# Scores of 64-wide heads by pairs on the two row halves of TensorE, even and odd heads in two banks

## The chip, the cores and the metric

The kernel runs on one core of one Trainium2 chip. The metric is the device time of one execution in microseconds (us), the median of three runs. The inputs are laid out on the host into the order in which the weights are read; everything that the reference computes is done in one launch.

## The reference

Two transformer-like blocks of two layers each follow each other on a sequence of 256 rows of width 1024, all in float32. Four of the attentions have heads of 64; the change touches three of them.

```python
# first block, per layer
y = hybrid_mixer(x, ...)        # A: chunked relative-position attention, 8 heads of 64
                                # B: latent attention, 8 heads of 64+32 (query/key 96 wide)
                                # C: forgetting attention, 8 heads of 64 (+2 columns of decay: 66)
x = layer_norm(alpha * x + y)
x = layer_norm(alpha * x + memory_cross_attention(x, mem, ...))   # 4 heads of 128
x = layer_norm(alpha * x + swiglu_ffn(x, ...))                    # hidden 2816

# second block, per layer; scale, shift and gate come from a modulation vector c
x = x + 0.5 * g1 * swiglu(norm(x))
h = norm(x)
o_a = stick_breaking(qa, ka, va)        # 4 heads of 64
o_d = dilated_mixture(qd, kd, vd)       # 4 heads of 64
o_h = hgrn2(qh, fh, ih, gh)             # 4 heads of 128, a gated linear recurrence
x = x + g2 * (concat(o_a, o_d, o_h) @ w_out)
x = x + 0.5 * g3 * swiglu(norm(x))

# the attentions that the change touches: A, stick_breaking, dilated_mixture
s = einsum('qhd,khd->hqk', q, k) * 64 ** -0.5 + bias_or_mask
p = softmax(s)                          # stick_breaking: exp of a cumulative sum instead
o = einsum('hqk,khd->qhd', p, v)
```

## The kernel before

The 256 rows are two threads of 128 (t = 0 and t = 1). Thread 0 runs ahead, thread 1 follows some weight tiles behind, so that each weight is loaded and split once and used by both. Every wide product is done in three float32r products: weights and activations are split into a rounded part and the rest (tiles `wh`, `wl`; for part of the weights both in the pool `E`; activations as two tiles of pool `S`), and `mm3` makes three products of 128x512 for each 128 rows of weight. Short float32 products (scores, values, the recurrence) are made directly; in the trace each of them is two MATMUL records and two LDWEIGHTS records, here called passes. A transpose is one record.

Nothing is issued in the order in which it is written. The program is recorded (`Recorder.add`), each operation gets a cost (`cost`, line 227), and a list scheduler (`listed`, line 282) sets the order of every engine: it works out a due time for every operation backwards from the order of TensorE's work, in which the duration of an operation that is not TensorE's is multiplied by `SLACK` (line 131), and then takes on each engine the ready operation that is due first, if the tiles it writes have room. Each thread has one PSUM bank `m` for the wide products and three banks `a` for everything else. So the scores of a head can be put between the wide products of the other thread, one matmul at a time.

`cost` gives a transpose 110 ns (`FP32`, line 524) and any other float32 product 220 ns.

The scores of heads of 64 (`scores`, line 770; called from `exponentials`, line 795, for attention A and the dilated attention, and from `stick`, line 1292): the transposed keys hold two heads in one block of 128 rows, the even head in rows 0 to 63, the odd one in rows 64 to 127. The queries (`queries`, line 855) are copied by ScalarE, half a tile at a time, into a tile of pool `E` that has one block per head and zeros in the other head's half (`zeroed`, line 863, four memsets on GpSimd), so that each score matmul runs over all 128 rows of the array, with the whole block of keys moving. Four score blocks of 128x128 fill one bank: four heads at t = 0, two heads with two key blocks each at t = 1. In the page these matmuls are `a<-S,E` with 128 rows and 128 columns; B and C have rows of 96 and 66 (`a<-S,S`) and are not touched.

The values (`values`, line 782) transpose the four probability blocks into one bank, ScalarE copies them, and then four matmuls `a<-T,S` each make 64 columns: the output of an even head stands in PSUM partitions 0 to 63, that of an odd head in 64 to 127. The softmax loop (line 825) holds one group of four blocks back while the next one's scores are made.

Of the kernel before, what the change touches and what calls it, by code (L numbers as in the profile page):

```python
# [130 lines left out]
SLACK = 1.5  # L131
# [16 lines left out]
class Recorder:  # L148
# [78 lines left out]
    def cost(self, op, name, out, src, kw):  # L227
# [9 lines left out]
        if op.eng == "PE":  # L237
            return (4.7 + 0.4406 * n, 0) if src[1].dtype == F32R else ((1 if name == "transpose" else 2) * FP32, 0)
# [290 lines left out]
class Program:  # L529
# [240 lines left out]
    def scores(self, t, nh, qT, kT):  # L770

        n = 4 // (t + 1)
        for b in range(0, nh, n):
            ps = self.ps()
            g = list(range(b, b + n))
            for i, h in enumerate(g):
                for u in range(t + 1):
                    o = (i * (t + 1) + u) * 128
                    self.nc.tensor.matmul(ps[:, o:o + 128], qT(h), kT(u, h), start=True, stop=True)
            yield g, ps  # L780

    def values(self, t, g, p, v, o, dv):


        nc = self.nc
        ps = self.blocks_T(p, 4)
        pT = self.tile("T", [128, 512])
        nc.scalar.copy(pT, ps)
        steps = [(i, u) for i in range(len(g)) for u in range(t + 1)]
        for i, u in sorted(steps, key=lambda k: k[::-1]) if dv < 128 else steps:  # L790
            h = g[i]
            b, r, c = (i * (t + 1) + u) * 128, h * dv % 128, h * dv // 128 * 128
            nc.tensor.matmul(o[r:r + dv, c:c + 128], v(u, h), pT[:, b:b + 128], start=u == 0, stop=u == t)

    def exponentials(self, t, nh, qT, kT, scale, bias=None, mult=None):
# [3 lines left out]
        for g, ps in self.scores(t, nh, qT, kT):  # L799
# [3 lines left out]
            s3 = s.rearrange("p (a b) -> p a b", a=n)  # L803
            p3 = ps.rearrange("p (a b) -> p a b", a=n)
# [20 lines left out]
    def softmax(self, t, nh, qT, kT, v, dv, scale, bias=None, mult=None):  # L825

        o, last = None, None
        for g, s in self.exponentials(t, nh, qT, kT, scale, bias, mult):
            yield
            if last:  # L830
                o = o or self.ps()
                self.values(t, *last, v, o, dv)
                yield
            last = g, s
        o = o or self.ps()
        self.values(t, *last, v, o, dv)
        yield
        return o

# [15 lines left out]
    def queries(self, t, ps, n, h0):  # L855

        nc = self.nc
        d = self.qz[t].rearrange("p (a two) b -> p a two b", two=2)
        p = ps[:, :n * 128].rearrange("p (a b) -> p a b", a=n)
        nc.scalar.copy(d[0:64, h0 // 2:h0 // 2 + n, 0, :], p[0:64])  # L860
        nc.scalar.copy(d[64:128, h0 // 2:h0 // 2 + n, 1, :], p[64:128])

    def zeroed(self, t):

        self.qz[t] = self.tile("E", [128, 1024]).rearrange("p (a b) -> p a b", a=8)
        d = self.qz[t].rearrange("p (a two) b -> p a two b", two=2)
        self.nc.gpsimd.memset(d[0:64, :, 1, :], 0.0)
        self.nc.gpsimd.memset(d[64:128, :, 0, :], 0.0)
# [57 lines left out]
    def mixer(self, l, t, xT):  # L926
# [4 lines left out]
        self.zeroed(t)  # L931
# [32 lines left out]
        if t == 0:  # L964
            st["rel"] = self.rel_bias(l)
        st["av", t] = self.copied((yield from self.wide(xT, main[2], 512, 2)), "S")
        rel = st["rel"]
        ya = self.beside(self.attention(
            t, 8, lambda h: self.qz[t][:, h, :], lambda u, h: st["ak", u][:, h // 2, :],
            lambda u, h: st["av", u][:, h * 64:h * 64 + 64], 64, 0.125,  # L970
            bias=lambda g: rel[g[0] // 4][:, g[0] % 4:g[0] % 4 + len(g), :128 * (t + 1)][:, :, ::-1]))
# [75 lines left out]
    def rel_bias(self, l):  # L1047
# [3 lines left out]
        for i in range(2):  # L1051
            b = self.tile("E", [128, 1024]).rearrange("p (a b) -> p a b", a=4)
            nc.sync.dma_start(b, bass.AP(tensor=src.tensor, offset=(l * 8 + i * 4) * 384, ap=[[1, 128], [384, 4], [1, 256]]))
# [36 lines left out]
    def cross(self, l, t, x):  # L1090
# [15 lines left out]
        for g, s in parts:  # L1106
            self.values(1, g, s, lambda u, h: st["xv", u][:, h * 128:h * 128 + 128], o, 128)
# [184 lines left out]
    def stick(self, t, kT, v):  # L1292
        nc, o, last = self.nc, None, None
        nk = 128 * (t + 1)
        for g, ps in self.scores(t, 4, lambda h: self.qz[t][:, h, :], kT):
            n = len(g)
            z, a, T = self.tile("T", [128, 512]), self.tile("T", [128, 512]), self.tile("T", [128, 512])
            nc.vector.scalar_tensor_tensor(z.rearrange("p (a b) -> p a b", a=n), ps.rearrange("p (a b) -> p a b", a=n), 0.125,
# [8 lines left out]
            yield  # L1307
            if last:
                o = o or self.ps()
                self.values(t, *last, v, o, 64)  # L1310
                yield
            last = g, z
        o = o or self.ps()
        self.values(t, *last, v, o, 64)
        yield
        return o
# [15 lines left out]
    def mixer2(self, l, t, xT):  # L1332
# [7 lines left out]
        st["k2", t], st["v2", t] = k2, v2  # L1340
        tasks = {}
# [3 lines left out]
        self.zeroed(t)  # L1345
# [23 lines left out]
        def dilated():  # L1369
            o = yield from self.softmax(  # L1370
                t, 4, lambda h: self.qz[t][:, 4 + h, :], lambda u, h: st["k2", u][:, 256 + h // 2 * 128:256 + h // 2 * 128 + 128],
                lambda u, h: st["v2", u][:, 256 + h * 64:256 + h * 64 + 64], 64, 0.125,
# [3 lines left out]
        def sticks():  # L1376
            o = yield from self.stick(t, lambda u, h: st["k2", u][:, h // 2 * 128:h // 2 * 128 + 128],
                                      lambda u, h: st["v2", u][:, h * 64:h * 64 + 64])
# [221 lines left out]
```

## Time and profile before

| | us |
|---|---|
| median of three runs | 2125.36 (2124.6 to 2126.13) |
| the profiled execution, its own time | 2126.53 |
| its span, first to last instruction | 2124.5 |
| TensorE busy in the span | 2087.4 (98%) |
| VectorE busy | 1567.6 (74%) |
| ScalarE busy | 1214.4 (57%) |
| GpSimd busy | 91.0 (4%) |
| granted TensorE clock, mean over the span | 1.00 |

The page sums the busy time of each engine over the span. A line of the trace names the engine, the operation, the tiles it writes and reads (`a<-S,E`: bank a from tiles of S and E), the rows and columns of the array that a matmul uses (`128*64`: 128 rows, 64 columns), the shape of the output, and its duration. Matmuls are pipelined: a record of 0.39 us overlaps with the next one, so what a matmul costs is read from the distance between starts, not from its duration.

### The profile page before, as it was taken

The page shows a single profiled execution, that of the slowest core. Times are in us where ns is not written, and L with a number is a line of the kernel's source. Part 1 is how long each engine was busy: PE and PEld are TensorE (multiplying, and loading weights), DVE is VectorE, ACT ScalarE, POOL GpSimd, SP SyncE. Part 2 cuts the span into 40 slices and gives each one's busy share as a digit, 9 for nine tenths or more (in the row PEclk, how much of TensorE's full clock was granted, in tenths as well). Part 3 has the DMA queues.
Part 4 walks back from the last instruction along what each step waited for, and adds up shares of the span by engine and source line. Part 5 has one row for each costly group of instructions (what it writes and reads, how often), then busy time and mean ns, then how long its engine had stood idle before and what let it go on. Part 6 is the DMA issues. An engine that isn't in the chain of part 4 may idle for free. (4 is left out here: it accounts for less than half of the span.)

```text
span 2124.5 us, 30068 instructions
## 1 busy us (share of the span) xinstructions
PE 2087.4 (98%) x10246; PEld 1690.9 (80%) x10246; DVE 1567.6 (74%) x3245; ACT 1214.4 (57%) x2538; POOL 91.0 (4%) x120
## 2 busy tenths in 40 slices
PE   8999999999999999999999999999999999999998
PEld 7788777888788878788878878878888887887887
DVE  5787888667888888877786678975566556997554
ACT  6977555444676755544454457764455445775442
POOL 0000200000000020000000000000000000000000
PEclk9999999999999999999999999999999999999999
DMA  7576776777767677688677652566656555256653
GB/s 265 162 251 217 245 252 218 253 253 257 250 218 256 215 253 256 214 265 267 227 243 246 234 182 96 160 189 189 192 176 188 171 187 185 71 162 204 187 185 105
DMA packets 150321, 443.20 MB, mean 209 GB/s; under 512 B 19208, under 2 KB 24344, under 8 KB 150168
## 3 DMA queue, kind: packets, MB, share of 16 engines
q1 hardware_dynamic: 150168, 441.29, 64.1%
q8 instruction: 80, 1.31, 0.2%
q14 instruction: 73, 0.60, 0.1%
HBM read 440.10 MB, written 1.12 MB: 208 GB/s over the span
## 5 line engine op out<-in xcount | busy, mean ns | idle before, releaser
L490 PE MATMUL m<-wh,S 128*128 128x512 f32 (+1 forms) x2944 | 932.0, 396 | 13.7 <-DVE S L490 4.6
L490 DVE TENSOR_TENSOR wl<-raw,wh 128x512 fp32r<-128x512 f32 (+1 forms) x982 | 652.4, 694 | 299.7 <-ACT wh L490 295.5
L490 ACT CAST wh<-raw 128x512 fp32r<-128x512 f32 (+1 forms) x982 | 563.9, 616 | 404.9 <-PE m L490 161.8
L490 PEld LDWEIGHTS m<-wh,S 128*128 128x128 f32 x2944 | 536.1, 188 | 137.4 <-DVE S L490 16.7
L490 PE MATMUL m<-wl,S 128*128 128x512 f32 (+1 forms) x1472 | 570.8, 392 | 0.0
L490 PE MATMUL m<-E,S 128*128 128x512 f32 x1308 | 346.0, 397 | 0.2
L490 PEld LDWEIGHTS m<-wl,S 128*128 128x128 f32 x1472 | 276.7, 188 | 56.8 <-issue 1.7
L490 PE MATMUL a<-wh,S 128*128 128x512 f32 x944 | 307.4, 399 | 3.8 <-ACT S L490 2.0
L490 DVE TENSOR_TENSOR E<-raw,E 128x512 fp32r<-128x512 f32 x334 | 218.5, 686 | 104.2 <-ACT E L490 84.7
L490 PEld LDWEIGHTS m<-E,S 128*128 128x128 f32 x1308 | 242.8, 188 | 53.7 <-DVE E L490 0.6
L490 ACT CAST E<-raw 128x512 fp32r<-128x512 f32 x334 | 192.8, 619 | 148.3 <-PE m L490 68.1
L490 PEld LDWEIGHTS a<-wh,S 128*128 128x128 f32 x944 | 173.2, 188 | 41.8 <-DVE S L490 3.7
L490 DVE SCALAR_TENSOR_TENSOR mr<-mr,c 128x512 f32<-128x512 f32 x288 | 192.7, 683 | 10.8 <-DMA mr<-in_w_mod 10.4
L490 PE MATMUL a<-E,S 128*128 128x512 f32 x648 | 184.7, 398 | 0.0
L490 PE MATMUL a<-wl,S 128*128 128x512 f32 x472 | 184.7, 394 | 0.0
L490 ACT CAST S<-a 128x256 fp32r<-128x256 f32 (+1 forms) x200 | 85.8, 429 | 126.2 <-PE a L490 125.0
L490 PEld LDWEIGHTS a<-E,S 128*128 128x128 f32 x648 | 119.7, 188 | 26.1 <-DVE E L490 0.6
L490 DVE TENSOR_TENSOR S<-a,S 128x256 fp32r<-128x256 f32 (+1 forms) x200 | 96.9, 490 | 46.0 <-ACT S L490 45.9
L490 PE MATMUL a<-c,T 128*128 128x128 f32 x652 | 120.8, 274 | 3.3 <-DVE T L490 2.4
L490 PEld LDWEIGHTS a<-c,T 128*128 128x128 f32 x652 | 84.7, 140 | 35.5 <-DVE T L490 6.3
L490 PEld LDWEIGHTS a<-wl,S 128*128 128x128 f32 x472 | 88.6, 188 | 19.3
L490 ACT ACTIVATE T<-m 128x256 f32<-128x256 f32 (+1 forms) x136 | 52.9, 389 | 78.8 <-PE m L490 78.4
(121 smaller groups left out, 1522.1 us busy)
## 6 DMA issues: line engine op xcount, KB each, us to landing
raw<-in_w_gu SPq DMA_DIRECT2D x264, 512.0 KB, 4.1
mr<-in_w_mod SPq DMA_DIRECT2D x288, 256.0 KB, 4.1
raw<-in_w_dn SPq DMA_DIRECT2D x132, 512.0 KB, 4.1
raw<-in_w_main SPq DMA_DIRECT2D x96, 512.0 KB, 4.1
raw<-in_w_in SPq DMA_DIRECT2D x56, 512.0 KB, 3.6
raw<-in_w_branch SPq DMA_DIRECT2D x24, 512.0 KB, 3.9
raw<-in_w_mo SPq DMA_DIRECT2D x16, 512.0 KB, 4.1
raw<-in_w_xkv SPq DMA_DIRECT2D x16, 512.0 KB, 4.2
```

The costliest lines, as they stand in the source:

```text
L490: ins = op.call(*args, **{a: real(v, op) for a, v in op.kw.items()})
```

## The change

Queries are no longer padded: the transposed queries of two heads are copied as one block of 128 rows into a tile of pool `S` (one ScalarE copy in place of two of half the rows), the memsets go, and a score matmul takes rows 0 to 63 or rows 64 to 127 of queries and keys (`half`). The compiler gives such a matmul a 64x128 tile of the array in place of the whole. Scores are made in two banks at once, one for the even heads and one for the odd heads, recorded alternately (`paired`). Softmax groups are therefore all-even or all-odd, the relative bias is loaded with even heads in one tile and odd heads in the other (the same two DMAs of the same size), and `values` takes an even and an odd group together and alternates between them. At t = 0 the stick-breaking and dilated attentions have two groups of two heads in place of one of four. The planner's numbers change too: a float32 matmul with 64 rows or 64 output partitions is now costed at 110 ns, and `SLACK` is 1.8.

```diff
@@ -128,7 +128,7 @@
 }
 OVERLAP = {"PE": 0, "ACT": 95, "DVE": 83, "POOL": 0, "SP": 0}
 TABLE = 1300
-SLACK = 1.5
+SLACK = 1.8
 ROUNDS = 1
 TRACE = 0
 WINDOW = 30
@@ -235,7 +235,7 @@
                 k *= c
             wide = max(n, k)
         if op.eng == "PE":
-            return (4.7 + 0.4406 * n, 0) if src[1].dtype == F32R else ((1 if name == "transpose" else 2) * FP32, 0)
+            return (4.7 + 0.4406 * n, 0) if src[1].dtype == F32R else ((1 if name == "transpose" or out.ap[0][1] == 64 or src[0].ap[0][1] == 64 else 2) * FP32, 0)
         if op.eng == "SP":
             parts = out.ap[0][1] if out.tensor.name in self.tiles else src[0].ap[0][1]
             return 60, 4 * n * parts
@@ -767,41 +767,52 @@
-    def scores(self, t, nh, qT, kT):
+    def scores(self, t, nh, qT, kT, paired):
         n = 4 // (t + 1)
-        for b in range(0, nh, n):
-            ps = self.ps()
-            g = list(range(b, b + n))
-            for i, h in enumerate(g):
+        if paired:
+            n = min(n, nh // 2)
+        step = 2 if paired else 1
+        for b in range(0, nh, n * step):
+            gs = [list(range(b + j, b + n * step, step)) for j in range(step)]
+            ps = [self.ps() for _ in gs]
+            for i in range(n):
                 for u in range(t + 1):
                     o = (i * (t + 1) + u) * 128
-                    self.nc.tensor.matmul(ps[:, o:o + 128], qT(h), kT(u, h), start=True, stop=True)
-            yield g, ps
-    def values(self, t, g, p, v, o, dv):
-        nc = self.nc
-        ps = self.blocks_T(p, 4)
-        pT = self.tile("T", [128, 512])
-        nc.scalar.copy(pT, ps)
-        steps = [(i, u) for i in range(len(g)) for u in range(t + 1)]
-        for i, u in sorted(steps, key=lambda k: k[::-1]) if dv < 128 else steps:
+                    for g, p in zip(gs, ps):
+                        self.nc.tensor.matmul(p[:, o:o + 128], qT(g[i]), kT(u, g[i]), start=True, stop=True)
+            yield from zip(gs, ps)
+    def values(self, t, groups, v, o, dv):
+        nc = self.nc
+        parts = []
+        for g, p in groups:
+            n = len(g) * (t + 1)
+            ps = self.blocks_T(p, n)
+            pT = self.tile("T", [128, 512])
+            nc.scalar.copy(pT[:, :n * 128], ps[:, :n * 128])
+            parts.append((g, pT))
+        steps = [(i, u, g, pT) for i in range(len(parts[0][0])) for u in range(t + 1) for g, pT in parts]
+        if len(parts) == 1 and dv < 128:
+            steps.sort(key=lambda k: (k[1], k[0]))
+        for i, u, g, pT in steps:
             h = g[i]
             b, r, c = (i * (t + 1) + u) * 128, h * dv % 128, h * dv // 128 * 128
             nc.tensor.matmul(o[r:r + dv, c:c + 128], v(u, h), pT[:, b:b + 128], start=u == 0, stop=u == t)
-    def exponentials(self, t, nh, qT, kT, scale, bias=None, mult=None):
+    def exponentials(self, t, nh, qT, kT, scale, bias=None, mult=None, paired=False):
         nc = self.nc
         nk = 128 * (t + 1)
-        for g, ps in self.scores(t, nh, qT, kT):
+        for g, ps in self.scores(t, nh, qT, kT, paired):
             n = len(g)
             s = self.tile("T", [128, 512])
             mx, sums, r = self.small(n), self.small(n), self.small(n)
-            s3 = s.rearrange("p (a b) -> p a b", a=n)
-            p3 = ps.rearrange("p (a b) -> p a b", a=n)
+            s3 = s[:, :n * nk].rearrange("p (a b) -> p a b", a=n)
+            p3 = ps[:, :n * nk].rearrange("p (a b) -> p a b", a=n)
             if bias is not None:
                 nc.vector.scalar_tensor_tensor(s3, p3, scale, bias(g), op0=ALU.mult, op1=ALU.add)
                 nc.vector.tensor_reduce(mx, s3, axis=AX.X, op=ALU.max, negate=True)
@@ -822,20 +833,27 @@
             nc.vector.tensor_tensor(s3, s3, r.unsqueeze(2).to_broadcast([128, n, nk]), op=ALU.mult)
             yield g, s
-    def softmax(self, t, nh, qT, kT, v, dv, scale, bias=None, mult=None):
-        o, last = None, None
-        for g, s in self.exponentials(t, nh, qT, kT, scale, bias, mult):
+    def weighted(self, t, parts, v, dv, paired):
+        o, lot, last = None, [], None
+        for g, s in parts:
             yield
-            if last:
+            lot.append((g, s))
+            if last and len(lot) == 1:
                 o = o or self.ps()
-                self.values(t, *last, v, o, dv)
+                self.values(t, last, v, o, dv)
+                last = None
                 yield
-            last = g, s
+            if len(lot) == 1 + paired:
+                last, lot = lot, []
         o = o or self.ps()
-        self.values(t, *last, v, o, dv)
+        self.values(t, last, v, o, dv)
         yield
         return o
+    def softmax(self, t, nh, qT, kT, v, dv, scale, paired=False, **k):
+        return self.weighted(t, self.exponentials(t, nh, qT, kT, scale, paired=paired, **k), v, dv, paired)
     def attention(self, t, nh, qT, kT, v, dv, scale, **k):
         o = yield from self.softmax(t, nh, qT, kT, v, dv, scale, **k)
@@ -854,18 +872,14 @@
     def queries(self, t, ps, n, h0):
-        nc = self.nc
-        d = self.qz[t].rearrange("p (a two) b -> p a two b", two=2)
-        p = ps[:, :n * 128].rearrange("p (a b) -> p a b", a=n)
-        nc.scalar.copy(d[0:64, h0 // 2:h0 // 2 + n, 0, :], p[0:64])
-        nc.scalar.copy(d[64:128, h0 // 2:h0 // 2 + n, 1, :], p[64:128])
-    def zeroed(self, t):
-        self.qz[t] = self.tile("E", [128, 1024]).rearrange("p (a b) -> p a b", a=8)
-        d = self.qz[t].rearrange("p (a two) b -> p a two b", two=2)
-        self.nc.gpsimd.memset(d[0:64, :, 1, :], 0.0)
-        self.nc.gpsimd.memset(d[64:128, :, 0, :], 0.0)
+        if self.qz[t] is None:
+            self.qz[t] = self.tile("S", [128, 4, 128])
+        self.nc.scalar.copy(self.qz[t][:, h0 // 2:h0 // 2 + n].rearrange("p a b -> p (a b)"), ps[:, :n * 128])
+    def half(self, x, h):
+        r = h % 2 * 64
+        return x[r:r + 64, h // 2]
     def wide_heads(self, src, nh, w):
@@ -928,7 +942,7 @@
         main = io["w_main"][l]
         if t == 0:
             self.deep, self.lag = 0, LAG
-        self.zeroed(t)
+        self.qz[t] = None
         merged = self.tile("X", [128, D])
         def gates(n):
@@ -964,11 +978,11 @@
         if t == 0:
             st["rel"] = self.rel_bias(l)
         st["av", t] = self.copied((yield from self.wide(xT, main[2], 512, 2)), "S")
-        rel = st["rel"]
+        rel, qA = st["rel"], self.qz[t]
         ya = self.beside(self.attention(
-            t, 8, lambda h: self.qz[t][:, h, :], lambda u, h: st["ak", u][:, h // 2, :],
-            lambda u, h: st["av", u][:, h * 64:h * 64 + 64], 64, 0.125,
-            bias=lambda g: rel[g[0] // 4][:, g[0] % 4:g[0] % 4 + len(g), :128 * (t + 1)][:, :, ::-1]))
+            t, 8, lambda h: self.half(qA, h), lambda u, h: self.half(st["ak", u], h),
+            lambda u, h: st["av", u][:, h * 64:h * 64 + 64], 64, 0.125, paired=True,
+            bias=lambda g: rel[g[0] % 2][:, g[0] // 2:g[0] // 2 + len(g), :128 * (t + 1)][:, :, ::-1]))
         ga = yield from gates(0)
@@ -1050,7 +1064,7 @@
         out = []
         for i in range(2):
             b = self.tile("E", [128, 1024]).rearrange("p (a b) -> p a b", a=4)
-            nc.sync.dma_start(b, bass.AP(tensor=src.tensor, offset=(l * 8 + i * 4) * 384, ap=[[1, 128], [384, 4], [1, 256]]))
+            nc.sync.dma_start(b, bass.AP(tensor=src.tensor, offset=(l * 8 + i) * 384, ap=[[1, 128], [768, 4], [1, 256]]))
             nc.gpsimd.memset(b[0:64, :, 0:64], NEG)
             out.append(b)
         return out
...
@@ -1289,13 +1303,14 @@
             nc.tensor.matmul(ps[:, s], st["kd"][:, s], e[:, s], start=True, stop=True)
         return [self.copied(ps, "S"), AT]
-    def stick(self, t, kT, v):
-        nc, o, last = self.nc, None, None
+    def stick(self, t, kT):
+        nc = self.nc
         nk = 128 * (t + 1)
-        for g, ps in self.scores(t, 4, lambda h: self.qz[t][:, h, :], kT):
+        for g, ps in self.scores(t, 4, lambda h: self.half(self.qz[t], h), kT, True):
             n = len(g)
-            z, a, T = self.tile("T", [128, 512]), self.tile("T", [128, 512]), self.tile("T", [128, 512])
-            nc.vector.scalar_tensor_tensor(z.rearrange("p (a b) -> p a b", a=n), ps.rearrange("p (a b) -> p a b", a=n), 0.125,
+            w = n * nk
+            z, a, T = (self.tile("T", [128, 512])[:, :w] for _ in range(3))
+            nc.vector.scalar_tensor_tensor(z.rearrange("p (a b) -> p a b", a=n), ps[:, :w].rearrange("p (a b) -> p a b", a=n), 0.125,
                                            self.mask(self.mask2, t, n), op0=ALU.mult, op1=ALU.add)
             self.softplus_parts(a, z)
             nc.vector.scalar_tensor_tensor(a, z, 0.0, a, op0=ALU.max, op1=ALU.add)
@@ -1304,16 +1319,7 @@
                 nc.vector.tensor_tensor_scan(T[:, c][:, ::-1], self.ones[:, :nk], a[:, c][:, ::-1], 0.0, op0=ALU.mult, op1=ALU.add)
             nc.vector.tensor_tensor(z, z, T, op=ALU.subtract)
             nc.scalar.activation(z, z, AF.Exp)
-            yield
-            if last:
-                o = o or self.ps()
-                self.values(t, *last, v, o, 64)
-                yield
-            last = g, z
-        o = o or self.ps()
-        self.values(t, *last, v, o, 64)
-        yield
-        return o
+            yield g, z
     def normed_heads(self, t, ps, g):
...
@@ -1368,14 +1375,14 @@
         def dilated():
             o = yield from self.softmax(
-                t, 4, lambda h: self.qz[t][:, 4 + h, :], lambda u, h: st["k2", u][:, 256 + h // 2 * 128:256 + h // 2 * 128 + 128],
-                lambda u, h: st["v2", u][:, 256 + h * 64:256 + h * 64 + 64], 64, 0.125,
+                t, 4, lambda h: self.half(self.qz[t], 4 + h), lambda u, h: self.half(k2s[u], 4 + h),
+                lambda u, h: st["v2", u][:, 256 + h * 64:256 + h * 64 + 64], 64, 0.125, paired=True,
                 bias=lambda g: self.mask(self.dil[:, 0], t, len(g)), mult=self.dil[:, 1] if t else self.dil[:, 1, 128:])
             self.split(o, 256, y, 256)
         def sticks():
-            o = yield from self.stick(t, lambda u, h: st["k2", u][:, h // 2 * 128:h // 2 * 128 + 128],
-                                      lambda u, h: st["v2", u][:, h * 64:h * 64 + 64])
+            o = yield from self.weighted(t, self.stick(t, lambda u, h: self.half(k2s[u], h)),
+                                         lambda u, h: st["v2", u][:, h * 64:h * 64 + 64], 64, True)
             self.split(o, 256, y, 0)
         def group(n):
```

On TensorE the planner's new order stands so in attention A of the first layer, thread 0, around the first half of its scores (a_114 is the bank of the first four heads, m the wide products). Before:

```order
L490 MATMUL m_110_513<-wh_443,S_6_168 128x512
L490 MATMUL a_114_517<-S_55_396,E_123 128x128
L490 MATMUL m_110_513<-wh_443,S_7_172 128x512
L490 MATMUL a_114_517<-S_55_396,E_123 128x128
L490 MATMUL m_110_513<-wl_451,S_6_168 128x512
L490 MATMUL a_114_517<-S_55_396,E_123 128x128
L490 MATMUL m_110_513<-wh_443,S_6_168 128x512
L490 MATMUL a_114_517<-S_55_396,E_123 128x128
L490 MATMUL m_110_513<-wh_443,S_7_172 128x512
```

In the change (a_114 is now the bank of the even heads, a_115 that of the odd ones):

```order
L490 MATMUL m_101_447<-wh_378,S_21_214 128x512
L490 MATMUL a_114_490<-S_55_390,S_36_295 128x128
L490 MATMUL m_101_447<-wh_378,S_22_223 128x512
L490 MATMUL a_115_493<-S_55_390,S_36_295 128x128
L490 MATMUL a_114_490<-S_55_390,S_36_295 128x128
L490 MATMUL a_115_493<-S_55_390,S_36_295 128x128
L490 MATMUL a_114_490<-S_55_390,S_36_295 128x128
L490 MATMUL m_101_447<-wl_386,S_21_214 128x512
L490 MATMUL a_115_493<-S_55_390,S_36_295 128x128
L490 MATMUL a_114_490<-S_55_390,S_36_295 128x128
L490 MATMUL a_115_493<-S_55_390,S_36_295 128x128
L490 MATMUL m_101_447<-wh_378,S_21_214 128x512
```

The first four scores stood one by one between wide products; the eight of both halves now stand as runs of one, four and three, with one wide product between two runs.

In the dilated attention of the second block's first layer, thread 1, before (a_3043 and a_3054 are the banks of its two groups, wh and wl weights of the following products, c_131 the identity of a transpose):

```order
L490 MATMUL a_3042_13978<-wh_13835,S_2777_13491 128x512
L490 MATMUL a_3043_13916<-S_2808_13469,E_12667 128x128
L490 MATMUL a_3043_13916<-S_2775_13312,E_12667 128x128
L490 MATMUL a_3043_13916<-S_2808_13469,E_12667 128x128
L490 MATMUL a_3042_13978<-wh_13835,S_2778_13705 128x512
L490 MATMUL a_3042_13978<-wl_13847,S_2777_13491 128x512
L490 MATMUL a_3051_13993<-c_131,T_2978_13629 128x128 x4
L490 MATMUL a_3054_14000<-S_2775_13312,E_12667 128x128
L490 MATMUL a_3054_14000<-S_2808_13469,E_12667 128x128
L490 MATMUL a_3054_14000<-S_2775_13312,E_12667 128x128
L490 MATMUL a_3054_14000<-S_2808_13469,E_12667 128x128
L490 MATMUL a_3041_13930<-wl_13864,S_2777_13491 128x512
```

In the change (a_3059 is the even bank, a_3060 the odd one, a_3056 takes the transposes of thread 0):

```order
L490 MATMUL a_3060_13970<-S_2775_13280,S_2905_13332 128x128
L490 MATMUL a_3059_13913<-S_2807_13422,S_2905_13332 128x128
L490 MATMUL a_3056_13974<-c_131,T_2984_13618 128x128
L490 MATMUL a_3060_13970<-S_2807_13422,S_2905_13332 128x128
L490 MATMUL a_3059_13913<-S_2775_13280,S_2905_13332 128x128
L490 MATMUL a_3056_13974<-c_131,T_2984_13618 128x128
L490 MATMUL a_3060_13970<-S_2775_13280,S_2905_13332 128x128
L490 MATMUL a_3059_13913<-S_2807_13422,S_2905_13332 128x128
L490 MATMUL a_3056_13974<-c_131,T_2984_13618 128x128
L490 MATMUL a_3060_13970<-S_2807_13422,S_2905_13332 128x128
L490 MATMUL a_3056_13974<-c_131,T_2984_13618 128x128
L490 MATMUL a_3055_13992<-wh_13821,S_2777_13546 128x512
```

Before, the scores stood as a run of three and a run of four here; in the change three pairs of one even and one odd score, and one single one, stand alternately with transposes that use the whole array.

## Rows read from the trace of the kernel before

**Rows 1.** The page: busy us (share of the span) and instructions of each engine.
```profile
PE 2087.4 (98%) x10246; PEld 1690.9 (80%) x10246; DVE 1567.6 (74%) x3245; ACT 1214.4 (57%) x2538; POOL 91.0 (4%) x120
```

**Rows 2.** Stretches: length, busy us (instructions) of PE, PEld, DVE, ACT, POOL; clock, DMA share, GB/s.
```profile
0.00:120.00 120.00, 112.23 (x604) 91.62 (x605) 83.44 (x199) 93.02 (x183) 6.39 (x20) 1.00 0.66 215
...
1250.00:1410.00 160.00, 155.37 (x841) 125.43 (x840) 141.17 (x316) 113.89 (x257) 14.97 (x17) 1.00 0.45 141
...
1780.00:1910.00 130.00, 126.37 (x699) 102.75 (x701) 118.58 (x273) 97.31 (x220) 9.61 (x9) 1.00 0.41 130
```

**Rows 3.** Groups by shape, TensorE: passes, then busy us, mean ns | idle before.
```profile
L490 PE MATMUL a<-T,S 128*64 128x128 f32 x384 | 34.6, 286 | 0.0
...
L490 PE MATMUL a<-S,E 128*128 128x128 f32 x192 | 27.5, 275 | 0.0
```

**Rows 4.** Timeline, TensorE, padded scores of attention A: start us, us, instruction, passes.
```profile
43.28 0.38 PE L490 MATMUL a<-S,E 128*128 128x128 f32 x2
43.42 0.48 PE L490 MATMUL m<-wh,S 128*128 128x512 f32 x1
43.74 0.38 PE L490 MATMUL a<-S,E 128*128 128x128 f32 x2
...
47.87 0.39 PE L490 MATMUL m<-wl,S 128*128 128x512 f32 x1
48.09 1.05 PE L490 MATMUL a<-S,E 128*128 128x128 f32 x8
48.90 0.71 PE L490 MATMUL m<-wh,S 128*128 128x512 f32 x2
49.45 0.39 PE L490 MATMUL m<-wl,S 128*128 128x512 f32 x1
```

**Rows 5.** Timeline, TensorE: four value matmuls of 64 columns in a run.
```profile
56.91 0.40 PE L490 MATMUL m<-wh,S 128*128 128x512 f32 x1
57.23 0.66 PE L490 MATMUL a<-T,S 128*64 128x128 f32 x8
57.82 0.50 PE L490 MATMUL m<-wh,S 128*128 128x512 f32 x1
58.16 0.39 PE L490 MATMUL m<-wl,S 128*128 128x512 f32 x1
```

**Rows 6.** Timeline, TensorE: value matmuls of 64 columns one by one.
```profile
90.17 0.40 PE L490 MATMUL m<-wh,S 128*128 128x256 f32 x2
90.41 0.28 PE L490 MATMUL m<-wl,S 128*128 128x256 f32 x1
90.52 0.39 PE L490 MATMUL m<-wh,S 128*128 128x256 f32 x2
90.85 0.43 PE L490 MATMUL a<-T,S 128*64 128x128 f32 x2
91.21 0.39 PE L490 MATMUL m<-wl,S 128*128 128x256 f32 x1
91.43 0.47 PE L490 MATMUL m<-wh,S 128*128 128x424 f32 x2
```

**Rows 7.** Timeline, TensorE: scores of attention B, 96 rows, not touched.
```profile
125.13 0.39 PE L490 MATMUL m<-wl,S 128*128 128x512 f32 x1
125.36 1.05 PE L490 MATMUL a<-S,S 96*128 96x128 f32 x8
126.17 0.71 PE L490 MATMUL m<-wh,S 128*128 128x512 f32 x2
```

**Rows 8.** Groups by shape, ScalarE: the copies of the queries, half a tile each.
```profile
L490 ACT COPY E<-a 64x256 f32<-64x256 f32 x16 | 5.9, 367 | 4.4 <-PE a L490 4.1
...
L490 ACT COPY E<-a 64x512 f32<-64x512 f32 x8 | 4.7, 582 | 1.0 <-PE a L490 0.8
```

**Rows 9.** Groups by shape, VectorE: operations 256 and 512 wide.
```profile
L490 DVE TENSOR_TENSOR T<-T,m 128x256 f32<-128x256 f32 x132 | 54.9, 417 | 35.4 <-ACT T L490 33.6
...
L490 DVE SCALAR_TENSOR_TENSOR T<-a,E 128x512 f32<-128x512 f32 x24 | 16.4, 682 | 2.7 <-PE a L490 2.5
```

More of the change, by code (lines that the diff above doesn't have):

```diff
@@ L1106, in cross @@
         for g, s in parts:
-            self.values(1, g, s, lambda u, h: st["xv", u][:, h * 128:h * 128 + 128], o, 128)
+            self.values(1, [(g, s)], lambda u, h: st["xv", u][:, h * 128:h * 128 + 128], o, 128)
         hi, lo = self.split(o, 512)
@@ L1340, in mixer2 @@
         st["k2", t], st["v2", t] = k2, v2
+        k2s = [st["k2", u].rearrange("p (a b) -> p a b", a=4) for u in range(t + 1)]
         tasks = {}
@@ L1344, in mixer2 @@
             self.masks2()
-        self.zeroed(t)
+        self.qz[t] = None
         def hgrn_all(qs, z):
```

## The prediction

> **What bounds the kernel now.** I read the sums per engine first: TensorE is busy 98% of the span, VectorE 74%, ScalarE 57%, GpSimd 4% [rows 1]. The granted clock is 1.00 in every stretch [rows 2], so it is at its upper level, 2.4 GHz, and no term below rests on a change of it. Then the table of stretches, for the places where the touched attentions stand: attention A of the first layer (0 to 120 us) and the second block's two mixers (1250 to 1410 and 1780 to 1910). In these mixers TensorE is busy 155.37 of 160 us and 126.37 of 130, which leaves 4.6 and 3.6 us; VectorE is next with 141 and 119 us [rows 2]. So TensorE's own time is the bound nearly everywhere, a microsecond added to it is mostly a microsecond of the kernel, and what matters is what a score matmul costs in TensorE's stream. That is read from the distance of starts in the timeline.
>
> **Prices from the timeline.** Two wide products of 512 columns take 0.46 us, 0.23 each. A lone padded score costs 0.23: from 43.28 to the next at 43.74 is 0.46, of which 0.23 is the wide product between [rows 4]. Four in a run (8 passes): they start on time (47.87 to 48.09), hold 0.81 until the next wide product, and the two wide starts after it are 0.55 apart instead of 0.46: 0.90, or 0.225 a score, 0.11 a pass [rows 4]. Scores of 96 rows do the same: 0.81 for 8 passes and no late start [rows 7]. So short of the whole array, fewer rows alone cost and save nothing.
>
> The value matmuls are what the trace has of a divided array: 64 columns, even and odd heads in turn. A run of four: it starts 0.32 after a wide product instead of 0.23 (0.09 late), holds 0.59, and the start after next is 0.34 away instead of 0.23 (0.11 late): 0.79 [rows 5]. The two halves do run together, 8 passes in 4 pass times, yet the run is only 0.11 cheaper than 0.90. A lone one: two 256-column products take 0.24 (90.17 to 90.41), so it should follow those of 90.52 at 90.76 and starts at 90.85 (0.09); it holds 0.36; the next product takes 0.22 instead of 0.12 (0.10): 0.55 [rows 6], against 0.23 for a lone undivided one. So going into the divided array and out of it costs 0.55 - 2 x 0.11 = 0.33 per run, whatever stands in the run, and each pass time in it 0.11. A run of eight alternating ones (8 pass times) comes to 0.79 + 4 x 0.11 = 1.23, against 1.80 undivided.
>
> **The change part by part.** *Scores.* All 96 score matmuls of A, stick-breaking and dilated attention (192 passes) [rows 3] now use half the rows. The trace shows no matmul with 64 rows. Bounds: the runs pair up and cost no way in or out (below), or they cost it and do not pair. I take the price of the columns' runs [rows 5, 6], the only rows of a divided array. How many runs there are is read from the new order: 42. They are 21 lone scores; 8 pairs of an even and an odd head; 7 runs of four pass times (two alternating fours, two threes, three pairs in the same half); one of six (three in the same half); and 5 of eight (four alternating eights, all in A at t = 1, and one four in the same half). That is 21 x 0.55 + 8 x 0.55 + 7 x 0.79 + 1.01 + 5 x 1.23 = 28.6 us. Before: 96 x 0.225 = 21.6. So +7.0 us. By place: A, with runs of 1, 4, 3, 8 and 8 a layer, 9.2 against 10.8, -1.6; the second block's mixers, where the planner puts them between wide products and transposes, 19.5 against 10.8, +8.7. The planner's new cost of 110 ns for a half matmul knows no way in or out; that is why it still breaks the runs.
>
> The Trainium skill (TensorEngine Tiling (Array Packing), Key Properties) says that changing the tiling mode, not just the tile, drains TensorE. The columns' rows agree, with 0.33 us a run; by that rule rows pay likewise, which gives the +7.0; by the page's theoretical factor of 2 for 64 rows (Overview) the scores would save 10.8.
>
> *Values.* Same 192 matmuls (384 passes) [rows 3]. Runs before: 46 of four pass times, 10 lone: 46 x 0.79 + 10 x 0.55 = 41.8. After: 28 of four, 17 of two, 8 of eight (sevens), one of six: 22.1 + 9.4 + 9.8 + 1.0 = 42.3. +0.5: what the longer lots save, the broken ones spend.
>
> *ScalarE.* 24 half-tile copies go, 8 x 0.58 + 16 x 0.37 = 10.6 us [rows 8]; 12 copies more of the same widths come (whole-height queries, narrower value tiles), 4 x 0.58 + 8 x 0.37 = 5.3. At 57% busy this is worth nothing directly. *VectorE.* At t = 0 the stick-breaking and dilated groups are two of 256 columns instead of one of 512: 12 operations are split, each 2 x 0.417 - 0.682 = 0.15 [rows 9], 1.8 us in all, in stretches where VectorE is 88 and 91% busy [rows 2]; covered by TensorE's longer work there, up to +1.8 if not. *GpSimd and DMA.* The memsets go from an engine with 91 us of work [rows 1]; the bias loads keep number and size. Nothing. *Space.* A pair of scores takes two of a thread's three banks a at once, and two tiles of pool E come free for one more in S. If a pair had to wait for its second bank as long as one VectorE pass over the first, 0.68 [rows 9], at 14 places (3 in A and 4 in the mixer, per layer), it were 9.6 us; wide products of the other thread fill such a wait, so I take 0 and leave it to the upper end.
>
> *The new due times.* `SLACK` 1.8 and the halved costs reorder everything. TensorE's idle time that this can take away is 8.3 us in the two mixers [rows 2] and 37 over the span [rows 1]; it can as well add some. The mixers' waits are for chains through VectorE and ScalarE, and TensorE's longer stream lets these catch up where it lies inside the chain. I take a third of the 8.3, -2.8, between 0 and -8.3.
>
> Sum: +7.0 + 0.5 - 2.8 = +4.7. The profiled execution took 2126.5 us (its span 2124.5, 2 us around it), 1.2 above the median of 2125.4: 2125.4 + 4.7 = 2130.
>
> **The rivals.** *Rows have no way in or out* (faster). If the weights of a half can be loaded while the whole array still streams, as an undivided score's are (no late start in rows 4), only pass times count: 132 x 0.11 = 14.5 against 21.6, so -7.1 + 0.5, and 2119. It decides below 0.17 us per run (7.1 / 42). For it: the padded scores' weight loads hide wholly. Against it: the columns' loads do not, in either run length [rows 5, 6], and a change of tile shape is all that they share with rows.
>
> *Rows pay the way and do not run together* (slower still). 192 x 0.11 + 42 x 0.33 = 35.0, +13.4, with the values 2139. For it: at 64 columns both the weights and the output are halved, at 64 rows each pass still loads 128 columns of weights and moves 128. Against it: the two halves read and write nothing in common. The Trainium skill (TensorE: Matmul & The Clock Gate, The mechanism) has weight loads overlap with running matmuls when their row groups differ; by that rule this rival falls, and no row here shows it. The wait for a second bank ends at the same time.
>
> *The waits give way* (no change). The price is right, but the later TensorE and the earlier due times hide all of the mixers' idle 8.3: 7.5 - 8.3 = -0.8, 2125. For it: ScalarE has 5 us less and TensorE's chains get more slack. Against it: the waits before a mixer's first transposes lie outside the scores.
>
> **How the numbers follow.** Forecast (2126 to 2135, around 2130) 0.40; waits give way (2125) 0.22; no way in or out (2119) 0.26; no running together (2139) 0.12. A measurement here tells about 0.2%, 4.3 us, from no change: faster is under 2121.1, slower over 2129.6. Slower: some 0.7 of the forecast's 0.40 (the new order can move it by 5 us) and the 0.12, 0.41 with a little of the waits' case. Faster: most of the 0.26, and a little of the waits' case: 0.25. Same: 0.34. The range goes from just under the fast case to between forecast and worst: 2118 to 2137; it leaves out some 0.2.
>
> **What would show it.** In the timeline after, a lone score `a<-S,S 64*128` between wide products should hold about 0.36 us and make the next start 0.1 late, and an alternating eight hold about 1.0. If halves pair, starts come two by two with 0.11 between the twos. If a lone score holds 0.22 and nothing starts late, the fast rival is right; if eights hold 1.8, the slow one. The rise should be in the mixers' stretches and none in the feed-forward ones; if TensorE's idle time there falls by 8 us, the waits gave way. A longer feed-forward stretch would be the planner's, and outside this argument.

## The result, and the profile after

The changed kernel takes 2137.0 us (median of four runs, 2136.2 to 2139.5) against 2125.7 beside it: a ratio of 1.0051, 95% interval 1.0039 to 1.0063, some 11 us slower. The forecast was 2130, slower by about 5; its range of 2118 to 2137 ends just at the result, and the time grew by more than twice what was forecast.

The page after, to be held against [rows 1]: TensorE is busy 8.2 us longer, in a span that is 9.9 longer; its idle time is 38.8 us instead of 37.1.

```profile
PE 2095.6 (98%) x10246; PEld 1689.5 (79%) x10246; DVE 1573.0 (74%) x3259; ACT 1206.4 (57%) x2535; POOL 83.4 (4%) x104
```

The same stretches as in [rows 2] (length, busy us of PE, PEld, DVE, ACT and POOL, granted clock, DMA share, GB/s): the idle time of TensorE in the two mixers is 3.6 and 3.7 us, 1.0 less together than before. But fewer instructions fit into the stretches (822 for 841, 674 for 699), so they hold other work; over 1250 to 1420 and 1770 to 1920 the idle time is 9.2 us against 8.6 before. It has hardly changed.

```profile
0.00:120.00 120.00, 112.82 (x623) 91.65 (x624) 87.81 (x218) 87.56 (x180) 5.62 (x16) 1.00 0.73 237
...
1250.00:1410.00 160.00, 156.38 (x822) 123.40 (x821) 137.69 (x312) 107.26 (x247) 10.89 (x12) 1.00 0.42 132
...
1780.00:1910.00 130.00, 126.32 (x674) 99.70 (x672) 111.37 (x258) 87.74 (x211) 10.39 (x11) 1.00 0.41 127
```

The groups by shape (count, then busy us and mean ns of one, then the idle time before them), for [rows 3]: the scores now stand with 64 rows. The rows of the weight loads (PEld), not shown before, have 136 ns for 64 columns and 186 for 128.

```profile
L490 PE MATMUL a<-T,S 128*64 128x128 f32 x384 | 35.4, 285 | 0.0
...
L490 PE MATMUL a<-S,S 64*128 64x128 f32 x192 | 25.8, 303 | 0.0
...
L490 PEld LDWEIGHTS a<-T,S 128*64 128x64 f32 x384 | 22.3, 136 | 16.8 <-issue 6.9 <-ACT T L490 5.9 <-ACT wh L490 2.3
...
L490 PEld LDWEIGHTS a<-S,S 64*128 64x128 f32 x192 | 17.8, 186 | 10.5 <-issue 7.7 <-ACT T L490 1.3 <-ACT S L490 0.3
```

What a run costs stands in the timeline of TensorE (start, us, instruction, passes). First comes a lone score between wide products of the second block, second a run of eight of attention A:

```profile
1328.36 0.63 PE L490 MATMUL m<-wh,S 128*128 128x512 f32 x2
1328.92 0.48 PE L490 MATMUL a<-S,S 64*128 64x128 f32 x2
1329.34 0.73 PE L490 MATMUL m<-wh,S 128*128 128x512 f32 x2
1329.91 0.62 PE L490 MATMUL m<-wl,S 128*128 128x512 f32 x2
```
```profile
62.93 0.39 PE L490 MATMUL m<-wl,S 128*128 128x512 f32 x1
63.24 1.16 PE L490 MATMUL a<-S,S 64*128 64x128 f32 x16
64.34 0.74 PE L490 MATMUL m<-wh,S 128*128 128x512 f32 x2
64.92 0.39 PE L490 MATMUL m<-wl,S 128*128 128x512 f32 x1
```

The lone score should start 0.46 after 1328.36, at 1328.82, and comes 0.10 late; it holds 0.42; the two starts after it are 0.57 apart instead of 0.46. That is 0.63 where a padded one cost 0.23 [rows 4], and more than the 0.55 of a lone value matmul [rows 6]. The eight: 0.31 instead of 0.23, 1.10 held, 0.58 instead of 0.46, together 1.30, against 1.80 undivided. So the halves run together, 16 passes in eight pass times of 0.11 (in the trace they start two by two, 7 ns apart), and the way in and out is some 0.40 a run. In the mixers most runs are too short for it. Here are three pairs and a lone one, with a transpose after each, in the dilated attention whose order was shown:

```profile
1375.09 0.49 PE L490 MATMUL a<-S,S 64*128 64x128 f32 x4
1375.51 0.33 PE L490 MATMUL a<-c,T 128*128 128x128 f32 x1
1375.77 0.49 PE L490 MATMUL a<-S,S 64*128 64x128 f32 x4
1376.19 0.33 PE L490 MATMUL a<-c,T 128*128 128x128 f32 x1
1376.45 0.49 PE L490 MATMUL a<-S,S 64*128 64x128 f32 x4
1376.87 0.33 PE L490 MATMUL a<-c,T 128*128 128x128 f32 x1
1377.13 0.49 PE L490 MATMUL a<-S,S 64*128 64x128 f32 x2
```

From pair to pair it takes 0.68 us; two padded scores (0.45) and a transpose (0.11) would need 0.56.

### The profile page after: what moved, and what is told of

It is laid out like the page before. It is cut to its first block, busy times and chain, and to the rows that moved or that the text cites. A ratio compares the mean times of both kernels' runs of the same rounds, so it can differ in the third digit from the quotient of the medians.

```text
span 2134.4 us, 30068 instructions
## 1 busy us (share of the span) xinstructions
PE 2095.6 (98%) x10246; PEld 1689.5 (79%) x10246; DVE 1573.0 (74%) x3259; ACT 1206.4 (57%) x2535; POOL 83.4 (4%) x104
## 5 line engine op out<-in xcount | busy, mean ns | idle before, releaser
L490 PE MATMUL m<-wh,S 128*128 128x512 f32 (+2 forms) x2944 | 936.8, 396 | 8.1 <-DVE S L490 4.6
L490 PE MATMUL m<-wl,S 128*128 128x512 f32 (+2 forms) x1472 | 569.8, 393 | 0.4 <-DVE wl L490 0.4
L490 PE MATMUL m<-E,S 128*128 128x512 f32 x1308 | 350.3, 398 | 3.3 <-DVE T L490 2.7
L490 DVE SCALAR_TENSOR_TENSOR mr<-mr,c 128x512 f32<-128x512 f32 x288 | 195.4, 689 | 10.6 <-DMA mr<-in_w_mod 10.4
L490 ACT CAST S<-a 128x256 fp32r<-128x256 f32 (+2 forms) x200 | 85.3, 428 | 95.6 <-PE a L490 94.9
L490 DVE TENSOR_TENSOR S<-a,S 128x256 fp32r<-128x256 f32 (+2 forms) x200 | 98.1, 493 | 34.3 <-ACT S L490 33.9
```

Of the source, the lines that this page charges most:

```text
L490: ins = op.call(*args, **{a: real(v, op) for a, v in op.kw.items()})
```

## The experiments

Theory A: the way into the divided array and out of it, paid once per run, is what the change costs, and where runs are broken it costs more than the halves save. Theory B: the new order and due times cost the time, and the halves cost nothing. Each ratio below is to the kernel before, run beside it, with its 95% interval. The expectations of the later runs (from the due times on) give the letters A and B a meaning of their own, which each of them states.

**The same order, undivided scores** (e1_whole).

```diff
     def half(self, x, h):
-        r = h % 2 * 64
-        return x[r:r + 64, h // 2]
+        return x[:, h // 2]
```

with the planner's cost of these matmuls left at 110 ns, so that its order stays the change's, matmul for matmul.

> The changed kernel's order on every engine, its copies and its groups kept as they are; only the 96 score matmuls use all 128 rows of the block again (left out: the heads of a pair are not told apart, each score is the sum of both). Theory A (the way into and out of the divided array is what the change costs): at the prices of the trace after, 0.62 us for a run of one or of one pair and 0.11 for each further pass time, the 42 runs cost 28.6 + 42 x 0.065 = 31.4 us; undivided 96 x 0.225 = 21.6, so 9.8 us less than the changed kernel: 2127 us, ratio to before 1.001. Theory B (the new order and due times cost the time, the divided matmuls nothing): as the changed kernel, 2137, ratio 1.005.

Measured: 2128.2 us, ratio 1.0003 (0.9994 to 1.0011). The score matmuls stand in TensorE's order where the 42 runs stood, but they make nothing late any more. (Where a start comes 0.31 or 0.32 after a wide product, that product itself had started early, as in [rows 4].) In its timeline the runs of one, four and three of attention A:

```profile
43.12 0.40 PE L491 MATMUL m<-wh,S 128*128 128x512 f32 x1
43.35 0.38 PE L491 MATMUL a<-S,S 128*128 128x128 f32 x2
43.49 0.48 PE L491 MATMUL m<-wh,S 128*128 128x512 f32 x1
43.81 1.05 PE L491 MATMUL a<-S,S 128*128 128x128 f32 x8
44.62 0.48 PE L491 MATMUL m<-wl,S 128*128 128x512 f32 x1
44.93 0.83 PE L491 MATMUL a<-S,S 128*128 128x128 f32 x6
45.52 0.71 PE L491 MATMUL m<-wh,S 128*128 128x512 f32 x2
```

and the same matmuls in the changed kernel:

```profile
41.80 0.39 PE L490 MATMUL m<-wh,S 128*128 128x512 f32 x1
42.11 0.49 PE L490 MATMUL a<-S,S 64*128 64x128 f32 x2
42.53 0.50 PE L490 MATMUL m<-wh,S 128*128 128x512 f32 x1
42.96 0.71 PE L490 MATMUL a<-S,S 64*128 64x128 f32 x8
43.60 0.50 PE L490 MATMUL m<-wl,S 128*128 128x512 f32 x1
44.04 0.71 PE L490 MATMUL a<-S,S 64*128 64x128 f32 x6
44.68 0.73 PE L490 MATMUL m<-wh,S 128*128 128x512 f32 x2
```

From the first row to the last it is 2.40 us undivided and 2.88 in halves, though the halves need fewer pass times. So the halves cost the whole of the change, 1.0051 - 1.0003 or some 10 us (9.8 expected; the two intervals leave about 3 us either way, and the two profiled spans lie 7.0 apart), and order, due times, copies and narrower groups together cost nothing that can be measured. Theory B falls.

As the order is the same matmul for matmul, the two traces can also be subtracted place by place, by the starts just before and just after each stretch of scores. In the two attentions A the halves gain 1.6 and 0.5 us; in the four stretches of the mixers they lose 3.1, 2.1, 3.1 and 2.1; over all the rest the two traces differ by 1.4. The prices of the runs say 1.1 gained and 10.9 lost.

**One block at a time** (e2_second_only, e3_first_only). Padded queries back in attention A, or in the second block's mixers.

From the edit of the first (`zeroed` and `padded` are the padding code of the kernel before):

```diff
-        self.qz[t] = None
+        self.zeroed(t)
...
-        self.queries(t, self.blocks_T(q, 4), 4, 0)
+        self.padded(t, self.blocks_T(q, 4), 4, 0)
...
-            t, 8, lambda h: self.half(qA, h), lambda u, h: self.half(st["ak", u], h),
...
+            t, 8, lambda h: qA[:, h, :], lambda u, h: st["ak", u][:, h // 2, :],
```

> The change in the second block's mixers alone, attention A of the first block with padded queries as before; planner's numbers as in the change. Theory A: 32 of the 42 runs, and nearly all the broken ones, are here; the trace after runs 12.4 us later over the two mixers than the trace before: 2138 us, ratio 1.006. Theory B (due times of the whole program): the same 2137 as the changed kernel, and so for the other half too.

> The change in attention A alone, the second block's mixers with padded queries as before; planner's numbers as in the change. Theory A: runs of 1, 4, 3, 8, 8 a layer cost 2 x 4.85 = 9.7 us instead of 10.8, and in the trace after the two stretches of attention A end 3.3 and 1.3 us earlier, of which 2 are lost again before the second block: 2123 us, ratio 0.999. Theory B: 2137 or so, ratio 1.005, as the due times are the change's.

Measured: in the second block alone 2142.5, ratio 1.0074 (1.0061 to 1.0086); in the first alone 2120.0, ratio 0.9967 (0.9955 to 0.9980), faster than before. The two parts have opposite signs, as theory A has it; by the ratios both went further than was expected, by some 3 and 5 us. With the mixers alone TensorE is busy 2099.4 us, 12.0 more than before, near the 10.9 of the prices. With A alone 7 us is more than the 1.1 of its runs: TensorE is busy 2085.3 of 2117.9 us, 2.1 less than before, and idle 4.5 less, 32.6. So most of this gain is waits that went, and which of them was not settled. Each of the two kernels has an order of its own; what the halves do in each place of the changed kernel is told by the subtraction above, not by these two times.

**Unbroken runs** (e4_sticky). The planner, while the array is divided, takes a ready matmul of the same division first, the other half before the same. The core of the edit:

```diff
+                    if e == "PE" and mode:
+                        for k in sorted((k for k in q if k[2].mode == mode), key=lambda k: (k[2].half == half, k)):
+                            q.remove(k)
+                            if room(k[2]):
+                                op = k[2]
+                                break
+                        heapq.heapify(q)
```

> The changed kernel with one rule more in the planner: while the array is divided, TensorE takes a ready matmul of the same division first, the other half before the same half. 16 score runs in place of 42, 48 value runs in place of 54. Theory A: scores 20.9 us by the prices after (two runs of twenty 3.04 each, four single-half fours 1.28, two fours 0.84, two sevens 1.28, two fives and two threes 1.06, two lone 0.62), 10.5 less than the change, values 39.9 instead of 42.3: 2124 us, ratio 0.999, a little faster than before or the same. Theory B (order and due times): no gain over the change, 2137, or worse, since urgent wide products wait behind the runs.

Measured: 2122.9, ratio 0.9979 (0.9970 to 0.9988). With 16 score runs in place of 42 the kernel is some 14 us faster than the changed one (12.9 by the prices of its score and value runs); TensorE is busy 10.6 us less and idle 2.5 less. The change is now a small gain. The twenty of attention A, between two wide products:

```profile
43.01 0.39 PE L503 MATMUL m<-wh,S 128*128 128x512 f32 x1
43.32 2.94 PE L503 MATMUL a<-S,S 64*128 64x128 f32 x40
46.19 0.50 PE L503 MATMUL m<-wh,S 128*128 128x512 f32 x1
46.53 0.40 PE L503 MATMUL m<-wl,S 128*128 128x512 f32 x1
```

0.31, 2.87 and 0.34 instead of 0.23, nothing and 0.23: 3.06 for twenty (3.04 by the prices), against 4.50 undivided. Sixteen of the twenty have a partner in the other half and four do not, so the run has 24 pass times.

**The due times alone** (e5_after_slack15, e6_before_slack18). One line each, `SLACK` exchanged between the two kernels.

> The changed kernel with SLACK 1.5 as before. Theory A (run count sets the time): the planner now makes 31 score runs in place of 42 and two lone value runs fewer; by the prices after (0.62 for a lone one or a pair, 0.11 per further pass time, 0.79 and 0.11 for values) scores 26.7 instead of 31.4, values 40.5 instead of 42.3, so 6.5 us less than the change: 2131 us, ratio 1.002. Theory B (the larger SLACK itself gained waits): 2137 or more.

> The kernel before with SLACK 1.8, padded queries and old costs. Theory A: no score runs of a divided array, values in 57 runs instead of 56, 42.6 us instead of 41.8: 2128 us, ratio 1.000, as far as due times do nothing by themselves. Theory B: due times are worth several us of waits, either way: 2121 or 2133.

Measured: the kernel before with 1.8 takes 2126.8, ratio 0.9999 (0.9990 to 1.0008): nothing. The changed one with 1.5 takes 2135.4, ratio 1.0040 (1.0027 to 1.0053): of the 6.5 us that the fewer runs should have given only about 2 came, and the two intervals overlap. TensorE is busy 2092.6 us in it, 3.0 less than in the change, and idle 39.5, 0.7 more. So the waits explain little of what is missing; the rest was not settled, and as a test of theory A this one is inconclusive.

**Whole lots** (e7_sticky_group, e8_first_sticky_group, e9_lots_first). In the changed kernel 14 of the 54 value runs are one lone matmul, whose partner's probabilities are not there yet. A second rule, beside that of the unbroken runs, begins a run only when every matmul recorded with it is ready, unless TensorE has nothing else. The core of the edit:

```diff
+                        if e == "PE" and k[2].mode and k[2].mode != mode and any(x.wait or x.ready > now for x in k[2].lot):
+                            early.append(k)
+                            continue
```

> The change everywhere, with two rules more in the planner: while the array is divided a ready matmul of the same division goes first, and a run is begun only when all matmuls of its lot are ready, unless TensorE has nothing else. 10 score runs in place of 42, 23 value runs in place of 54. Theory A: scores 16.8 us (before 21.6), values 29.7 (before 41.8), so 16.9 less than before with the waits as they were: 2110 us, ratio 0.992. Theory B: what the runs save comes back as waits of ScalarE and VectorE for later scores and values: 2123, no better than the sticky rule alone.

> The same two rules, with the change in attention A alone and padded queries in the second block. 4 score runs of a divided array, 8.6 us instead of 10.8; 25 value runs, 29.7 us instead of 41.8: 14.3 less than before, 2112 us, ratio 0.993. Theory A says about 2 us slower than the same rules with the change everywhere, since in unbroken runs the second block's pairs pay too (8.2 against 10.8); theory B (halves in the second block's mixers lose in any form, by groups of half width and two banks at once) says faster than that by some us.

Measured: with the change everywhere 2139.7, ratio 1.0059 (1.0045 to 1.0073), a miss by 30 us; with the change in attention A alone 2114.1, ratio 0.9946 (0.9933 to 0.9958), near the 2112 expected and the fastest here. In the first of the two TensorE is busy less than before and idle 59.9 us:

```profile
PE 2078.0 (97%) x10246; PEld 1692.8 (79%) x10246; DVE 1572.4 (74%) x3259; ACT 1207.2 (56%) x2538; POOL 88.8 (4%) x104
```

Its stretches in the first of the second block's mixers (length, busy us of PE, PEld, DVE, ACT, POOL, granted clock, DMA share, GB/s), and the timeline of TensorE there:

```profile
1325.00:1331.00 6.00, 5.81 (x42) 4.19 (x40) 3.40 (x8) 3.78 (x9) 0.00 (x0) 1.00 0.66 220
1331.00:1336.00 5.00, 1.89 (x9) 1.69 (x10) 5.00 (x11) 4.91 (x12) 0.00 (x0) 0.80 0.44 129
1336.00:1340.00 4.00, 1.15 (x5) 0.58 (x4) 3.87 (x10) 1.97 (x5) 0.00 (x0) 0.50 0.26 101
1340.00:1344.00 4.00, 3.23 (x14) 3.06 (x14) 3.31 (x8) 2.74 (x9) 0.00 (x0) 0.50 0.30 57
```
```profile
1330.41 0.40 PE L515 MATMUL m<-wl,S 128*128 128x512 f32 x1
1332.90 0.44 PE L515 MATMUL a<-c,T 128*128 128x128 f32 x2 [2.09 <-ACT T L515]
1334.54 2.04 PE L515 MATMUL a<-T 128*128 128x128 f32 x8 [1.21 <-DVE T L515]
1339.44 0.69 PE L515 MATMUL a<-c,T 128*128 128x128 f32 x2 [2.85 <-ACT T L515]
```

TensorE has run out of wide products and waits for tiles from ScalarE and VectorE. VectorE is busy 8.87 of the 9 us from 1331; ScalarE waits in turn, between 1326 and 1345 for 3.9 us, for weight tiles to land. TensorE's clock is then granted at half, 1.2 GHz. Two causes were possible: that lots were waited for in the mixers, or that TensorE was 10 us ahead of the other engines. The next run has the second rule in the first block alone (`self.nc.lots = False` at the head of `mixer2`, and no lot for matmuls recorded after it).

> As the run before the last (both rules, change everywhere, 2139.7), but a lot is waited for in the first block alone; in the second block's mixers only the first rule (same division first) holds. Their order is then that of the sticky run but for when it begins. Theory A (waiting for whole lots in the mixers starves TensorE, which then falls to half clock): the first block keeps its 10 us gain, the mixers lose 2.5 and 1.8 us as in the sticky run, no half clock in them: 2121 us, ratio 0.997. Theory B (TensorE being 10 us ahead of the other engines, or pairs as such, starves it there): 2135 to 2140, with half clock again near 1335 us.

Measured: 2118.3, ratio 0.9958 (0.9944 to 0.9971). In the same stretches TensorE works, at full clock:

```profile
1331.00:1336.00 5.00, 4.62 (x25) 3.41 (x25) 4.91 (x10) 3.24 (x7) 0.00 (x0) 1.00 0.15 37
1336.00:1340.00 4.00, 4.00 (x27) 3.61 (x26) 4.00 (x9) 3.63 (x13) 0.00 (x0) 1.00 0.77 232
```

So it was the waiting for lots in the mixers, together with the halved scores: with undivided scores there (2114.1) the value matmuls of the mixers wait for their lots too, and the clock stays at 1.00 in both mixers.

2118.3 against 2114.1 does not show that halves lose in the mixers in any form, what the expectation for the second of the three runs called theory B. Without the second rule the mixers have the runs of e4_sticky: twelve score runs, 12.3 us by the prices against 10.8 undivided, and 14 value runs in place of 8, some 3 us more. That is about as much as was measured (4 us, or 2.6 by the ratios, whose intervals overlap). The six unbroken score runs that would gain there, 8.2 us by the prices, stood only in the kernel that starved; whether they pay without that was not tried.

## Why the prediction was right, and where not

The direction and the mechanism were right and the size was not: +11 measured, +4.7 forecast. That the result is still at the very end of the range is luck: that end was set between the forecast and a rival that proved wrong.

*What bounds the kernel.* Right: of the 9.9 us that the profiled span grew, TensorE is busy 8.2.

*The price of a run.* The mechanism was right, the size too small. Rows pay for going in and out as columns do, and pair as columns do; but a run costs 0.62 to 0.63, not 0.55, and eight 1.29 to 1.30, not 1.23. The likely reason is the first weight load, which nothing hides: 186 ns for 128 columns, 136 for 64, a difference of 0.05; no run varies the load alone, so this is not shown. With some 0.065 more in each of the 42 runs the scores come to 31.4, so the term is +9.8 instead of +7.0; e1_whole measured some 10.

*By place.* Right in sign and roughly in size: -1.6 for A and +8.7 for the mixers, where the subtraction at the same order gives -2.1 and +10.4, and the rise stands where it was to stand. The -7 and +16 of the two kernels with one part each hold more than the halves, most of it for A in waits.

*Values, ScalarE, VectorE, bias loads.* +0.5 and nothing: with the scores undivided the rest of the change is 1.0003 of the kernel before, within its interval of no change.

*The waits.* Wrong. A third of the mixers' idle 8.3 us was to be taken by the longer stream, -2.8. The idle time there stayed within 1 us of what it was, and over the span it rose by 1.7. This is the larger part of the miss: +9.8 + 0.5 + 1.7 would have given 2137. The halves are not what brings it: with the scores undivided in the same order the idle time is 39.3 us, as long. What it comes from was not settled.

*The rivals.* No way in or out: refuted by the late starts and by e1_whole. No running together: refuted by 16 passes in 1.10. The waits give way: refuted by the idle time. Two rules of the Trainium skill were weighed. That changing the tiling mode drains TensorE (TensorEngine Tiling (Array Packing), Key Properties) agrees with the trace, with 0.40 us a run for 64 rows. That matmuls in different row groups overlap (TensorE: Matmul & The Clock Gate, The mechanism) agrees with it too, with 16 passes in eight pass times.

## What to carry to other kernels

A divided array pays only in unbroken runs: here a run of n alternating 64-row float32 matmuls costs 0.62 + 0.11 x (n - 2) us against 0.225 x n undivided, so by these prices two lose 0.17 and four gain 0.06, and the run of twenty, of which four did not alternate, was measured to gain 1.4. A scheduler that is not told of the way in and out breaks the runs, here into 42 for 96 matmuls; let it keep a run together, but not hold its first matmul back for the last where the chain behind it is short of time. Judge such a change by stage: at the same order it gained 2 us in one place and lost 10 in another, and the sum hid both.

## What the runs showed of the hardware

A start that waits for a change of division costs the same whether 64 columns or 64 rows are taken (0.1 late on either side), and scores of 96 rows cost none [rows 7]. Two passes in different halves of the rows take one pass time of 0.11, with starts 7 ns apart, although each brings its own 128 columns of weights. And TensorE, after waits of 2.09 and 1.21 us (busy 1.89 of the 5 us from 1331), ran at 1.2 GHz: the eight passes from 1334.54 took 2.04 us where eight took 1.05 [rows 4], so a wait cost more than its length.
